# Differential-attention heads: rotary straight from PSUM, mask and row extreme in one VectorE operation, one sub-norm per head

## The chip, the cores and the metric

The program runs on one core of a Trainium2 chip. The metric is device microseconds of one execution. Five instruction queues run side by side and wait for one another through semaphores: TensorE (PE; its weight loads are listed apart as PEld), VectorE (DVE), ScalarE (ACT), GpSimd (POOL) and SyncE (SP, which here only issues DMAs). Every queue works strictly in its own order: an instruction that waits holds up all that stands behind it.

## The reference, cut to what matters

One decoder layer over 1024 tokens and a model width of 2048, all in float32. After an RMSNorm one input projection gives q, k, v and gate columns of two groups of eight heads: stick-breaking heads (not changed here) and differential heads. For a differential head:

```python
dq = partial_rope(df_q.reshape(qk_shape), pos)   # (B, S, 8 heads, 2, 64): two q/k pairs per head
dk = partial_rope(df_k.reshape(qk_shape), pos)   # rotates the first 16 of 64 dims: 8 with 8
s = einsum('bqhcd,bkhcd->bhcqk', qi, k) * 64 ** -0.5
pr = softmax(where(kpos <= qpos, s, -inf), axis=-1)
a = pr[:, :, 0] - lam * pr[:, :, 1]
df_out = rmsnorm(a @ v, subln_g, 1e-5) * (1 - lambda_init)
mixed = concat([sb_out * silu(sb_g), df_out * silu(df_g)])
```

An output projection, a gated per-layer embedding and a final RMSNorm follow.

## The kernel before, in words

The input comes in transposed, features on partitions, with the order of tokens turned round, so that the keys that a block of 128 queries may see lie at the end of a row. The tokens are worked in two halves of 512. A float32 product is made of three matmuls on a high and a low part of each operand (high·high, high·low, low·high), in the type fp32r. Before the heads, one stage computes the v and gate columns and puts them into DRAM (`vg_d`); behind the heads follow the output projection and the gate stage. Neither is touched.

The heads run in a fixed order: for half 1 the eight differential heads (8 to 15) and then the eight stick-breaking heads, then the same for half 0. Half 1 sees its own 512 keys alone; half 0 sees 1024. For each head `unit` makes the q and k columns: four weight pieces, each of eight groups of three matmuls of 512 columns, into two PSUM accumulators `acc0` (q) and `acc1` (k). A *tick* passes behind every group, 32 of them a head. All other work of a head hangs on ticks: `side.add([(t, fn)])` puts a step t ticks ahead, and steps that have come due are written into the program there. So the attention of one head is interleaved with the projection matmuls of the next, and **the order of the matmuls on PE is fixed in writing by tables of ticks** (`SC` for scores, `TT` for the transposes and the mixing, `ROPE`, `VGD`, `DF0`, `DF1`, `LM`, `LN`, `LAST`); on the other engines a scheduler orders the steps. PE never overtakes a matmul whose operand is late.

The way of a differential head, with the lines of the profile:

- **Rotation.** `taken` scales each accumulator by the row norm (and q by 64^-0.5) on DVE into SBUF (L1605 for q, L1609 for k). Only 16 of every 64 rows rotate, so SP DMAs gather the first 32 rows of both pairs of q and of k into one tile `rot` (L1612). DVE exchanges rows 0-7 with 8-15 (`stream_shuffle`, L1617), multiplies by sine and cosine (L1622, L1623) and adds (L1625). SP DMAs carry the rotated rows back (L1629).
- **Split and placing.** ACT casts to the high part (L1633); SP DMAs put the halves of it where the score matmuls want them: `q`, `qz` (the other 64 rows zero) and `k` (both copies) (L1636). DVE subtracts for the low part (L1642, L1646); two DMAs place q's low half (L1644). These are 18 DMA issues on SP per head, in the queue that also carries the weight pieces (L183, L184) and v and gate (L1513).
- **Scores.** Two matmuls give q·k (L338, L341; half 1: L427, L430) into a PSUM tile `z`; between them PE adds the causal mask as a bf16 matmul of an identity with a mask block (L340, L429). DVE reduces each row to minus its maximum (L388, L440), ACT takes exp with the row sum (L397, L444), DVE and ACT form the difference of the two softmaxes (L402 to L410, L447 to L452).
- **Mixing.** `turn` transposes the weights on PE into PSUM `tp` (L487), ACT and DVE split them (`awh` L505, `awl` L510, `lead` L504/L509), `mix` multiplies by v (L530 to L535) into PSUM `av`. `tp`, `av`, v's transpose and the sum of squares `msq` share one PSUM ring of two buffers.
- **Sub-norm.** For each half of a head's 512 queries PE sums squares into `msq` (L576, L577), ACT takes ln and exp of it (L604, L605), DVE makes one Newton step (L608 to L610, the first of them still reading `msq`) and scales (L611).
- **v and gate.** `load_vg` (L1513) reads them from DRAM; DVE multiplies both by the row norm (L1650), ACT makes the sigmoid of the gate.

In the order of the program of half 0, SP's queue stands so before the change, behind one weight piece (`whi`, `wlo`):

```order
L1612 DMA rot<-qk 32x512 x2
L304 DMA comb_d<-sg 128x512
L1629 DMA qk<-rot 32x512 x4
L183 DMA whi<-whi_d 128x1024
L184 DMA wlo<-wlo_d 128x1024
L1513 DMA vf<-vg_d 128x512
L1513 DMA gf<-vg_d 128x512
L1636 DMA q<-sw 64x512
L1636 DMA qz<-sw 64x512
```

The write-back of the rotated rows stands ahead of a weight piece and of v and gate.

Of the kernel before, what the change touches and what calls it, by code (L numbers as in the profile page):

```python
# [34 lines left out]
SC = ((20.5, 21, 23.5, 25.5, 29.5, 31.5, 34.0, 37.0), (24.5, 27, 34, 41))  # L35
TT = ((32, 44, 30.0), (35.5, 52, 33))
DGAP = (3, 6.5)
DF0 = (1, 1, 1.5, 3.5, 5.5)
DF1 = (1, 1.0, 3, 5, 6.5)
LV = ((2.0, 2.5), (1, 2))  # L40
LT = ((1, 1), (1, 2.0))
LM = ((0.5, 2.0, 3, 5), (1, 2, 4, 6))
LN = ((1, 4.0), (1, 4.5))
PRIO = 300
NORM_LAT = ((8, 7.0), (13, 11))
XLAT = 5
SBB = ((20, 20, 15, 16.0, 15, 16.5, 16.5, 16.0), (20, 9, 5.5, 4, 5.0, 6.0, 5.5, 4.0))
SBS = ((-1, 3.5, 15.5, 23.5), (0.5, 2, 7.5, 11.5))
SBT = ((15, 31, 11), (14.0, 27.5, 10.5))
SGAP = (3.5, 6.5)  # L50
SBL = ((1.5, 3, 6.0), (1, 3, 5.0))
SVG = ((18, 40.5, 42, 43, 49), (33.5, 34.5, 39.0, 40.0, 48.0))
ROPE = ((3.5, 4.0, 6.0, 10.0, 11.6, 12.5, 15.0), (6.5, 7, 9.5, 12.5, 12.6, 13.5, 14))
VGD = ((40, 47, 48, 49.0, 51.0), (37.5, 47.5, 47.5, 47.5, 55.5))
# [4 lines left out]
LAST = 2, 4.5  # L59
MASKPE = True  # L60
# [9 lines left out]
def _body(ctx, nc, tc, ap):  # L70
# [13 lines left out]
    masks = const.tile([P, 2, P], BF16, name="masks", tag="masks")  # L84
    identb = const.tile([P, P], BF16, name="identb", tag="identb")
# [14 lines left out]
    def consts_late():  # L100
        V.tensor_scalar(subg, subg, 1.0 - LAM0, None, op0=ALU.mult)
        V.tensor_copy(identb, ident)
# [207 lines left out]
    def attention(at, pz, half, hd, q, qz, K, KL, VV, sg, vg, state):  # L310
# [9 lines left out]

        def scores(c, rb):
# [5 lines left out]
            for ki, k in enumerate(K):  # L327
# [9 lines left out]
                else:  # L337
                    T.matmul(o, q[:, c, rs], k[:, c, c0:HALF], start=True, stop=False)  # L338
                    if ki == 0:
                        T.matmul(z[:, rs], identb, masks[:, 1, :], start=False, stop=False, skip_group_check=True)  # L340
                    T.matmul(o, qz[:, c, rs], KL[:, ki, c0:], start=False, stop=True)  # L341

            def masked():
                mask = masks[:, 0, :]
# [10 lines left out]
        def weights(rb, c):  # L355
# [30 lines left out]
            def top():  # L386
                mx = at.tile([P, 1], F32, name="mx", tag="mx", bufs=8)
                V.reduce_max(mx, z[:, vw], axis=AX.X, negate=True)  # L388
                side.later(DF0[2], partial(one, mx))

            def one(mx):
# [5 lines left out]
                A.activation(et[:, vw], z[:, vw], AF.Exp, bias=mx[:, 0:1], accum_out=l)  # L397
# [20 lines left out]
        def pairs(rb):  # L418
# [6 lines left out]
            for c in range(2):  # L425
                o = z[:, c, c0:]
                T.matmul(o, q[:, c, rs], k[:, c, c0:HALF], start=True, stop=False)  # L427
                if MASKPE:
                    T.matmul(z[:, c, rs], identb, masks[:, 1, :], start=False, stop=False, skip_group_check=True)  # L429
# [5 lines left out]
            def masked():  # L435
                mask = masks[:, 1:2, :].broadcast_to([P, 2, P])
                V.tensor_tensor(z[:, :, rs], z[:, :, rs], mask, op=ALU.add)

# [133 lines left out]
        def norm(pr):  # L572
# [5 lines left out]
            if hd == ORDER1[H - 1]:  # L578
# [4 lines left out]
                if pr == 0:  # L583
                    return
# [1843 lines left out]
```

## Time and profile before

| what | value |
|---|---|
| median of 3 runs | 2469.01 us (2468.71 to 2471.68) |
| the profiled execution | 2460.97 us, span 2459.2 us |
| granted clock over the span | 0.99 |
| busy share of the span | PE 96%, PEld 79%, DVE 71%, ACT 45%, POOL 14% |
| differential heads of half 1 (first to last q evacuated) | 644.1 to 869.1 us |
| stick-breaking heads of half 1 and the seam to half 0 | 869.1 to 1139.0 us |
| differential heads of half 0 | 1139.0 to 1431.1 us |
| stick-breaking heads of half 0 | 1431.1 to about 1800 us |

A row of the timeline has the start, the duration, the engine and line, the operation with its operands, and in brackets how long the engine had sat idle before it and what released it. A matmul's end is modelled, so that back-to-back matmuls overlap in the rows; what one costs is read from the distance of the starts.

### The profile page before, as it was taken

The page shows a single profiled execution, that of the slowest core. Times are in us where ns is not written, and L with a number is a line of the kernel's source. Part 1 is how long each engine was busy: PE and PEld are TensorE (multiplying, and loading weights), DVE is VectorE, ACT ScalarE, POOL GpSimd, SP SyncE. Part 2 cuts the span into 40 slices and gives each one's busy share as a digit, 9 for nine tenths or more (in the row PEclk, how much of TensorE's full clock was granted, in tenths as well). Part 3 has the DMA queues.
Part 4 walks back from the last instruction along what each step waited for, and adds up shares of the span by engine and source line. Part 5 has one row for each costly group of instructions (what it writes and reads, how often), then busy time and mean ns, then how long its engine had stood idle before and what let it go on. Part 6 is the DMA issues. An engine that isn't in the chain of part 4 may idle for free.

```text
span 2459.2 us, 33022 instructions
## 1 busy us (share of the span) xinstructions
PE 2358.3 (96%) x11230; PEld 1936.3 (79%) x11230; DVE 1754.9 (71%) x2954; ACT 1109.5 (45%) x2086; POOL 333.5 (14%) x496
## 2 busy tenths in 40 slices
PE   9999999999999989998999999999999999999997
PEld 7888878888777768886777778888878787778876
DVE  7589776666366767765677777767877886677688
ACT  6343243333244555443555555545632434532453
POOL 1211122223000000000010101110111222011000
PEclk9999999999999999999999999999999999999998
DMA  7797589999889888778687877667888899898965
GB/s 261 243 368 251 185 239 295 290 276 281 280 263 292 274 283 292 269 246 257 192 220 209 223 208 212 190 203 234 211 219 199 262 273 279 292 326 284 317 210 176
DMA packets 276457, 619.88 MB, mean 252 GB/s; under 512 B 33664, under 2 KB 45952, under 8 KB 276288
## 3 DMA queue, kind: packets, MB, share of 16 engines
q1 hardware_dynamic: 197328, 424.53, 53.2%
q0 software_dynamic: 59664, 158.10, 25.3%
q10 hardware_dynamic: 19296, 35.14, 4.1%
q8 instruction: 88, 1.44, 0.2%
q14 instruction: 81, 0.66, 0.1%
HBM read 374.37 MB, written 222.30 MB: 243 GB/s over the span
## 4 chain that ended last, share of the span: by engine, by line
PE 63%; DMA 16%; DVE 13%; ACT 4%; issue 3%; SPq 2%; DVEq 0%; ACTq 0%
PE pbc L726 6%; PE pbc L727 6%; PE pbc L728 6%; PE acc L262 5%; PE acc L264 5%; PE acc L263 5%; DMA rot<-qk 3%; PE pa L726 2%; PE pa L727 2%; PE pa L728 2%; PE tp L487 2%; DMA gf<-vg_d 2%; DMA q<-qk 1%; DMA wraw<-w_gate 1%; DMA wraw<-w_out 1%
## 5 line engine op out<-in xcount | busy, mean ns | idle before, releaser
L817 ACT CAST wpr<-T 128x512 fp32r<-128x512 f32 x208 | 125.4, 620 | 437.8 <-DVE T L782 358.3
L262 PE MATMUL acc<-xh,whi 128*128 128x512 f32 x768 | 314.2, 409 | 0.1
L264 PE MATMUL acc<-xh,wlo 128*128 128x512 f32 x768 | 303.0, 395 | 2.8 <-DVE wlo L195 2.5
L263 PE MATMUL acc<-xl,whi 128*128 128x512 f32 x768 | 301.5, 393 | 0.0
L264 PEld LDWEIGHTS acc<-xh,wlo 128*128 128x128 f32 x768 | 144.8, 189 | 37.1 <-DVE wlo L195 3.8
L263 PEld LDWEIGHTS acc<-xl,whi 128*128 128x128 f32 x768 | 145.7, 190 | 24.2
L262 PEld LDWEIGHTS acc<-xh,whi 128*128 128x128 f32 x768 | 145.7, 190 | 24.0 <-ACT whi L190 0.5
L817 ACT CAST wpr<-wraw 128x512 fp32r<-128x512 f32 x144 | 88.3, 616 | 153.5 <-DMA wraw<-w_vg 45.8
L831 DVE TENSOR_TENSOR wpr<-T,wpr 128x512 fp32r<-128x512 f32 x208 | 142.7, 686 | 11.3 <-ACT wpr L817 7.4
L950 POOL DMA_DIRECT2D vg_d<-hc x120 | 86.8, 724 | 331.1 <-DVE hc L1191 203.9
L510 DVE TENSOR_TENSOR awl<-tp,awh 128x256 fp32r<-128x256 f32 (+1 forms) x160 | 92.3, 577 | 46.0 <-ACT awh L505 45.8
L831 DVE TENSOR_TENSOR wpr<-wraw,wpr 128x512 fp32r<-128x512 f32 x144 | 97.8, 685 | 38.1 <-ACT wpr L817 38.0
L726 PE MATMUL pbc<-cS,wpr 128*128 128x512 f32 x288 | 112.2, 389 | 0.8 <-DVE u L1247 0.8
L728 PE MATMUL pbc<-cS,wpr 128*128 128x512 f32 x288 | 112.0, 389 | 0.0
L727 PE MATMUL pbc<-cS,wpr 128*128 128x512 f32 x288 | 112.0, 389 | 0.0
L505 ACT CAST awh<-tp 128x256 fp32r<-128x256 f32 (+1 forms) x160 | 80.4, 502 | 52.7 <-PE tp L487 44.9
L373 DVE TENSOR_TENSOR_SCAN st<-pt 128x511 f32<-128x511 f32 (+3 forms) x64 | 86.7, 1354 | 17.9 <-ACT pt L366 17.6
L388 DVE TENSOR_REDUCE mx<-z 128x1 f32<-128x1024 f32 (+3 forms) x64 | 65.2, 1018 | 32.7 <-PE z L341 32.6
L535 PE MATMUL av<-awl,v 128*128 128x256 f32 x256 | 74.9, 293 | 11.1 <-DVE awl L510 10.9
L366 ACT ACTIVATE pt<-z 128x512 f32<-128x512 f32 (+3 forms) x64 | 41.8, 653 | 88.8 <-DVE z L349 85.0
L397 ACT ACTIVATE et<-z,mx 128x1024 f32<-128x1024 f32 (+3 forms) x64 | 60.8, 952 | 31.9 <-DVE mx L388 31.9
L533 PE MATMUL av<-awh,v 128*128 128x256 f32 x256 | 72.6, 284 | 1.3 <-ACT awh L505 1.2
(579 smaller groups left out, 6798.7 us busy)
## 6 DMA issues: line engine op xcount, KB each, us to landing
wlo<-wlo_d SPq DMA_DIRECT2D x94, 512.0 KB, 5.2
whi<-whi_d SPq DMA_DIRECT2D x74, 512.0 KB, 4.1
wraw<-w_vg SPq DMA_DIRECT2D x130, 256.0 KB, 4.9
vg_d<-hc POOLq DMA_DIRECT2D x120, 256.0 KB, 5.8
wraw<-w_in SPq DMA_DIRECT2D x54, 512.0 KB, 5.4
wraw<-w_gate SPq DMA_DIRECT2D x92, 256.0 KB, 5.8
wraw<-w_out SPq DMA_DIRECT2D x72, 256.0 KB, 5.0
wlo_d<-wlo SPq DMA_DIRECT2D x34, 512.0 KB, 3.6
```

Of the source, the lines that this page charges most:

```text
L262: T.matmul(acc[c], hi[:, k2, kh, c, :], xh, start=first, stop=False)
L263: T.matmul(acc[c], hi[:, k2, kh, c, :], xl, start=False, stop=False)
L264: T.matmul(acc[c], lo[:, k2, kh, c, :], xh, start=False, stop=last)
L373: V.tensor_tensor_scan(st[:, off + 1:nkey], pt[:, off:nkey - 1], pt[:, off:nkey - 1], initial=1.0, op0=ALU.mult, op1=ALU.bypass)
L505: A.copy(wh[:, o, :], tp[:, o, :])
L510: V.tensor_tensor(wl[:, o, :], tp[:, o, :], wh[:, o, :].bitcast(F32), op=ALU.subtract)
L726: T.matmul(o, wh[:, w], xh, start=start and k == 0, stop=False, skip_group_check=True)
L727: T.matmul(o, wh[:, w], xl, start=False, stop=False, skip_group_check=True)
L728: T.matmul(o, wl[:, w], xh, start=False, stop=k == 3, skip_group_check=True)
L817: A.copy(t[:, 0], src)
L831: V.tensor_tensor(t[:, 1], src, t[:, 0].bitcast(F32), op=ALU.subtract)
L950: G.dma_start(vg_d[hf, blk, u], o, **(dict(accum_op=ALU.add) if ph else {}))
```

## The change

The table that `rope` loads (`cs`) is multiplied once per half by the row norm (two operations on 128x1024), so the rotation needs no norm of its own. For each head and each of q and k, DVE multiplies the accumulator by the cosine table straight from PSUM, shuffles the accumulator straight from PSUM, multiplies the shuffled copy by the sine table (zero where nothing rotates) and adds. All 128 rows go through, no row is moved. ACT writes q's and k's high parts in their places itself, 64 rows at a time (`high`, `spread`), and DVE writes q's low halves in their places (`low`). The 18 SP DMAs of a head are gone.

The mask matmul is gone too, and the scale 64^-0.5 with it out of q: one VectorE operation with an accumulator output (`tensor_tensor_reduce`) adds a mask row to the scores, multiplies by -64^-0.5, writes back to PSUM and gives the row's minimum; exp then runs with scale -1. In the order of the program it is two rows, the operation and the reading of its accumulator. In half 1 there is one for each of the two pairs, where one reduction took both.

The sub-norm takes both halves of a head together: ACT copies each `msq` out, then ln, exp and a square on 512 columns, and three DVE operations on 512 columns replace eight on 256.

The tick tables are other ones throughout; the table `VGD` asks for v and gate (first entry) and uses them (second and third) at other ticks than before.

```diff
-SC = ((20.5, 21, 23.5, 25.5, 29.5, 31.5, 34.0, 37.0), (24.5, 27, 34, 41))
-TT = ((32, 44, 30.0), (35.5, 52, 33))
+SC = ((6.5, 7, 9.0, 11.5, 15.5, 17.5, 20.0, 21.5), (10.5, 10.5, 15.5, 22.5))
+TT = ((19, 31, 17.5), (20.5, 36.5, 18))
...
-ROPE = ((3.5, 4.0, 6.0, 10.0, 11.6, 12.5, 15.0), (6.5, 7, 9.5, 12.5, 12.6, 13.5, 14))
-VGD = ((40, 47, 48, 49.0, 51.0), (37.5, 47.5, 47.5, 47.5, 55.5))
+CST = (19.5, 20)
+ROPE = ((-1.4, 1.5, 3.0, 3.5, 2.7, 4.5, 6.0, 7.0), (-1.9, -1, 0, 1, 0.20000000000000018, 2, 3, 4))
+VGD = ((31, 37, 37.0, 39.0, 41.0), (22.5, 32.5, 35.5, 37.0, 45.0))
...
+        def masked_top(z, n, mx):
+            V.tensor_tensor_reduce(z, z, mwide[:, 0:n], -DF_SCALE, 3.0e38, ALU.add, ALU.min, mx)
...
-                    if ki == 0:
-                        T.matmul(z[:, rs], identb, masks[:, 1, :], start=False, stop=False, skip_group_check=True)
...
-                V.reduce_max(mx, z[:, vw], axis=AX.X, negate=True)
+                masked_top(z[:, vw], nkey - off, mx)
...
-                A.activation(et[:, vw], z[:, vw], AF.Exp, bias=mx[:, 0:1], accum_out=l)
+                A.activation(et[:, vw], z[:, vw], AF.Exp, bias=mx[:, 0:1], scale=-1.0, accum_out=l)
...
-                V.reduce_max(mx, z[:, :, vw], axis=AX.X, negate=True)
+                for c in range(2):
+                    masked_top(z[:, c, vw], HALF - off, mx[:, c:c + 1])
...
+            if pr == 0:
+                sqs["both"] = [ev.tile([P, HALF], F32, name=nm, tag="sq", bufs=2) for nm in ("msqs", "rsub")]
+            m, r = sqs["both"]
+            side.later(LN[half][0], lambda: A.copy(m[:, ms_], msq))
+            if pr == 0:
+                return
...
             def step():
-                V.scalar_tensor_tensor(sq, msq, SUB_EPS, rs_, op0=ALU.add, op1=ALU.mult)
-                V.scalar_tensor_tensor(sq, sq, -0.5, rs_, op0=ALU.mult, op1=ALU.mult)
-                V.scalar_tensor_tensor(rs_, sq, 1.5, rs_, op0=ALU.add, op1=ALU.mult)
-                V.tensor_tensor(sg[:, ms_], sg[:, ms_], rs_, op=ALU.mult)
+                V.scalar_tensor_tensor(sg, sg, -0.5, r, op0=ALU.mult, op1=ALU.mult)
+                A.activation(r, r, AF.Square)
+                V.scalar_tensor_tensor(m, m, SUB_EPS, r, op0=ALU.add, op1=ALU.mult)
+                V.scalar_tensor_tensor(sg, m, -3.0, sg, op0=ALU.add, op1=ALU.mult)
...
+                if hd == (ORDER0, ORDER1)[half][0]:
+                    side.add([(CST[half], lambda cs=cs, rstd=rstd: V.tensor_tensor(cs, cs, rstd.rearrange("p (a n) -> p a n", a=1).broadcast_to([P, 2, HALF]), op=ALU.mult))])
...
-                            V.scalar_tensor_tensor(f, acc[c], DF_SCALE, rstd, op0=ALU.mult, op1=ALU.mult)
-                            V.tensor_tensor(f, acc[c], rstd, op=ALU.mult)
-                        for b in range(2):
-                            m = 64 * c + 32 * b
-                            nc.sync.dma_start(fs["r"].bitcast(F32)[m:m + 32, :], f[64 * b:64 * b + 32, :])
+                        f, sw = [t.bitcast(F32) for t in fs[c]]
+                        V.tensor_tensor(f, acc[c], cs[:, 0, :], op=ALU.mult)
+                        V.stream_shuffle(sw, acc[c], SWAP)
...
+                    def turned(c, fs=fs):
+                        f, sw = [t.bitcast(F32) for t in fs[c]]
+                        V.tensor_tensor(sw, sw, cs[:, 1, :], op=ALU.mult)
+                        V.tensor_tensor(f, f, sw, op=ALU.add)
+                    def high(c, fs=fs, qk=qk):
+                        f = fs[c][0].bitcast(F32)
+                        if c:
+                            A.copy(fs[1][1], f)
+                        for b, r in enumerate(rows):
+                            A.copy(qk[c][r, b, :], f[r])
+                    def low(c, fs=fs, qk=qk):
+                        f = fs[c][0].bitcast(F32)
+                        if c:
+                            V.tensor_tensor(qk["kl"][:, 0, :], f, fs[1][1].bitcast(F32), op=ALU.subtract)
                             return
                         for b, r in enumerate(rows):
+                            V.tensor_tensor(qk[0][rows[1 - b], b, :], f[r], qk[0][r, b, :].bitcast(F32), op=ALU.subtract)
+                    def spread(c, fs=fs, qk=qk, store_k=store_k, state=state):
+                        f = fs[c][0].bitcast(F32)
                         state.add("qk"[c])
+                        for b, r in enumerate(rows):
+                            if c:
+                                A.copy(qk[1][rows[1 - b], b, :], f[r])
+                            else:
+                                A.copy(qk["qz"][r, b, :], f[r])
+                        if c:
+                            store_k()
```

Three places of the new order, with the line numbers of the changed file. SP's queue in half 0 at the place that was shown before (`comb_d` is a store of an earlier head's result; L1491 loads v and gate):

```order
L184 DMA wlo<-wlo_d 128x1024
L304 DMA comb_d<-sg 128x512
L183 DMA whi<-whi_d 128x1024
L184 DMA wlo<-wlo_d 128x1024
L1491 DMA vf<-vg_d 128x512
L1491 DMA gf<-vg_d 128x512
```

No DMA of the rotation stands ahead of v and gate now, but the weight piece still does.

DVE's queue in half 1 from the k accumulator on (`acc_6302`) to the last thing that k's scores need (`kl`):

```order
L1587 TENSOR_TENSOR qk<-acc_6302,cs 128x512
L1588 STREAM_SHUFFLE sw<-acc_6302 128x512
L1608 TENSOR_TENSOR q<-qk,q 64x512 x2
L1592 TENSOR_TENSOR sw<-sw,cs 128x512
L1593 TENSOR_TENSOR qk<-qk,sw 128x512
L1622 TENSOR_TENSOR vf<-vf,ssa 128x512
L1605 TENSOR_TENSOR kl<-qk,sw 128x512
L1622 TENSOR_TENSOR gf<-gf,ssa 128x512
```

and ACT's queue at the same place:

```order
L499 CAST awh<-tp 128x512
L1600 CAST q<-qk 64x512 x2
L1617 CAST qz<-qk 64x512 x2
L1598 CAST sw<-qk 128x512
L1600 CAST k<-qk 64x512 x2
L1615 CAST k<-qk 64x512 x2
```

The work that SP's DMAs did now stands in these two queues, and `kl` stands behind the use of v (`vf`). On PE the first score matmul of this head now follows the last matmul of its k accumulator after 33 matmuls of 512 columns, six of 256 and three transposes; before, after 75 of 512, 21 of 256, 14 transposes and four mask matmuls. In half 0 it is 21 of 512, 17 of 256 and 11 transposes, from 69 of 512, 42 of 256, 26 transposes and three mask matmuls.

PE's queue at the scores of half 0, before the change:

```order
L338 MATMUL z<-k,q 128x384
L340 LDWEIGHTS identb
L340 MATMUL z<-masks,identb 128x128
L341 MATMUL z<-kl,qz 128x384
L338 MATMUL z<-k_10263,q 128x512
L341 MATMUL z<-kl,qz 128x512
```

and after it:

```order
L341 MATMUL z<-k,q 128x384
L342 MATMUL z<-kl,qz 128x384
L341 MATMUL z<-k_10146,q 128x512
L342 MATMUL z<-kl,qz 128x512
L524 MATMUL av<-lead,v 128x256 x2
```

Two instructions of PE's queue are gone at each of 128 places.

121 lines of the change are left out of this document (32 added, 89 removed).

## The prediction

> **What bounds the kernel now.** I read the page first: PE is busy nearly all the time, and the chain of waits that ended last lies on PE for the most part, then on DMA.
>
> ```profile
> PE 2358.3 (96%) x11230; PEld 1936.3 (79%) x11230; DVE 1754.9 (71%) x2954; ACT 1109.5 (45%) x2086; POOL 333.5 (14%) x496
> PE 63%; DMA 16%; DVE 13%; ACT 4%; issue 3%; SPq 2%; DVEq 0%; ACTq 0%
> ```
>
> So only what takes matmul time off PE, or idle time ahead of a matmul, can move the end. The windows by stage (length; busy of PE, PEld, DVE, ACT, POOL; granted clock; DMA) show where PE is not full: the stages with differential heads.
>
> ```profile
> core 0: us, PE busy (x) PEld busy (x) DVE busy (x) ACT busy (x) POOL busy (x), PEclk, DMA share, GB/s
> 200.00:250.00 50.00, 50.00 (x222) 41.39 (x222) 45.05 (x73) 19.75 (x34) 7.36 (x14) 1.00 0.71 229
> 644.10:869.10 225.00, 210.19 (x1042) 167.77 (x1040) 137.67 (x293) 97.31 (x256) 11.62 (x21) 0.98 0.89 276
> 1180.20:1431.10 250.90, 237.55 (x1265) 191.02 (x1263) 181.41 (x358) 134.75 (x267) 23.24 (x33) 1.00 0.77 213
> ```
>
> In half 1 seven head intervals fill 225.0 us (32.1 a head, DVE 19.7 of it); in half 0 six steady heads fill 250.9 (41.2 a head by the spacing of their q evacuations, DVE 29.8 of it). PE lacks 14.8 and 13.4 us there; the early stage shows PE full with DVE at 45.05 of 50.
>
> Third, PE's waits between 644 and 1500 us (who waited for whom: us in total, times, longest):
>
> ```profile
> PE tp L487 <- DVE sqv L608: 13.2, 13, 4.0
> PE z L427 <- DMA q<-qk: 10.8, 6, 5.1
> PE av L535 <- DVE awl L510: 10.2, 16, 2.1
> PE z L338 <- DMA q<-qk: 8.6, 6, 6.7
> PE av L530 <- DVE lead L509: 5.3, 3, 2.6
> ```
>
> Three kinds: scores waiting for the DMAs that place q and k (19.4), transposes waiting for a PSUM buffer that `msq` holds until the Newton step L608 (13.2), the mixing waiting for DVE (15.5). The timeline tells what lies behind them:
>
> ```profile
> 1157.56 0.62 ACT L1633 CAST sw<-qk 128x512 fp32r<-128x512 f32 x1 [11.28 <-DMA qk<-rot]
> 1167.86 0.80 PE L338 MATMUL z<-k,q 128*128 128x512 f32 x1 [6.73 <-DMA q<-qk]
> 915.35 0.90 PE L487 MATMUL tp<-ident,et 128*128 128x128 f32 x3 [3.99 <-DVE sqv L608]
> 1236.96 2.42 SPq L1629 DMA_DIRECT2D qk<-rot  x4
> 1241.02 0.43 SPq L1513 DMA_DIRECT2D gf<-vg_d  x1
> 1248.54 0.69 DVE L1650 TENSOR_TENSOR gf<-gf,ssa 128x512 f32<-128x512 f32 x1 [1.24 <-DMA gf<-vg_d]
> 1248.01 0.28 PE L533 MATMUL av<-awh,v 128*128 128x256 f32 x1
> 1248.12 0.28 PE L534 MATMUL av<-awh,v 128*128 128x256 f32 x1
> 1249.89 0.39 PE L535 MATMUL av<-awl,v 128*128 128x256 f32 x1 [1.49 <-DVE awl L510]
> ```
>
> The rotation's round trips stop ACT for 11.28 us and then PE for 6.73. In half 0 the mixing waits for a DVE that waits for the gate `gf`, landing 7.5 us after its issue (1241.02 to 1248.54). After the longest waits PE also runs slow for a while:
>
> ```profile
> 1167.00:1174.00 7.00, 6.14 (x17) 4.41 (x18) 1.95 (x2) 1.21 (x2) 0.00 (x0) 0.58 0.31 114
> 911.00:920.00 9.00, 4.75 (x14) 3.28 (x13) 7.67 (x17) 5.00 (x13) 1.07 (x2) 0.64 0.60 218
> ```
>
> A clock of 0.58 over 7.0 us loses 2.9 us, 0.64 over 9.0 us 3.2.
>
> **The change part by part. The mask matmul.** 128 of them go.
>
> ```profile
> 1299.94 0.33 PE L338 MATMUL z<-k,q 128*128 128x384 f32 x1
> 1300.11 0.23 PE L340 MATMUL z<-masks,identb 128*128 128x128 bf16 x1
> 1300.15 0.42 PE L341 MATMUL z<-kl,qz 128*128 128x384 f32 x1
> 1300.41 0.39 PE L338 MATMUL z<-k,q 128*128 128x512 f32 x1
> 1300.63 0.39 PE L341 MATMUL z<-kl,qz 128*128 128x512 f32 x1
> L340 PE MATMUL z<-masks,identb 128*128 128x128 bf16 x64 | 15.0, 234 | 0.0
> L429 PE MATMUL z<-masks,identb 128*128 128x128 bf16 x64 | 14.9, 233 | 0.0
> ```
>
> By starts, L338 on 384 columns takes 0.17 us, the mask 0.04, and the L341 behind it, on as many columns, 0.26 instead of 0.17: the mask costs 0.04 + 0.09 = 0.13. At 0.12 to 0.13 each, 128 make 15.4 to 16.6; I take **-15.4**.
>
> The busy sums of the two rows would give 29.9. [...]
>
> ```profile
> L340 PEld LDWEIGHTS <-identb 128*128 128x128 bf16 x64 | 6.3, 98 | 10.7 <-issue 10.0
> ```
>
> [...]
>
> **The DMA waits.** With the 18 DMAs per head the wait of 19.4 goes. Each of its 12 waits hides a further 0.16, because a matmul of 0.39 in the rows starts its successor after 0.23: 1.9. Clock after the two longest (5.1, 6.7): two times 2.9, near 6. Together **-27**.
>
> **The PSUM wait.** `msq` is freed by a copy one tick behind its matmul, no longer by L608 on a busy DVE: 13.2, hidden 13 x 0.16 = 2.1, clock near 5 (3.2 at 915, less at the shorter ones): **-20**.
>
> **The wait for v and gate** stays, I think. SP no longer holds them behind the write-back, but they follow a weight piece still, and half 0's table asks 6 ticks ahead (31 to 37) where it asked 7 (40 to 47). Six ticks of a 37 us head are 6.9 us, against the 7.5 seen. The row L1650 still stands before DVE's next split in half 0, and PE's mixing behind that. I take 0; the bounds are -18.5 (15.5 and 19 x 0.16: all goes) and +6 (8 steady heads by 0.7, the difference).
>
> **DVE and ACT per head.** The rows that price it (mean ns behind the comma):
>
> ```profile
> L1609 DVE TENSOR_TENSOR qk<-acc,ssa 128x512 f32<-128x512 f32 x15 | 10.3, 687 | 1.7 <-PE acc L264 1.4
> L1617 DVE STREAM_SHUFFLE sw<-rot 128x512 f32<-128x512 f32 x16 | 11.8, 735 | 0.1
> L1623 DVE TENSOR_TENSOR rot<-rot,cs 128x512 f32<-128x512 f32 x16 | 11.0, 685 | 0.0
> L388 DVE TENSOR_REDUCE mx<-z 128x1 f32<-128x1024 f32 x16 | 19.6, 1225 | 30.3 <-PE z L341 30.3
> L378 DVE TENSOR_TENSOR bt<-st,bt 128x1023 f32<-128x1023 f32 x8 | 9.7, 1216 | 0.0
> L402 DVE RECIPROCAL l<-l 128x1 f32<-128x1 f32 x64 | 9.9, 155 | 2.5 <-ACT et L397 2.5
> L608 DVE SCALAR_TENSOR_TENSOR sqv<-msq,rsub 128x256 f32<-128x256 f32 x28 | 11.6, 414 | 0.0
> L1633 ACT CAST sw<-qk 128x512 fp32r<-128x512 f32 x16 | 9.9, 619 | 41.1 <-DMA qk<-rot 41.0
> ```
>
> Rotation: 8 operations become 11, +2.1 us. Sub-norm: 8 x 0.414 become 3 x 0.69, -1.2. The new masked minimum is not in the trace. It streams two operands like L378 and reduces like L388; both run 1024 columns in 1.22, so at one pass it costs what L388 did, plus an accumulator read (near 0.16, the shortest DVE row): 8 x 0.16 = +1.3 a head. At two passes it costs their sum, 2.44. One pass is my value, since a single operand stream sets both rows. DVE then needs 29.8 + 2.2 = 32.0 of a half 0 head of about 37 (86%), and some 22.5 of 28 in half 1: under the 90% at which PE was full in the early stage. ACT gains 7 casts (+4.3) and 1 us of norm per head, on 45% busy; its cover is PE's stream. The two multiplications of the table (1.2 us each) hide under a head's matmuls, at tick 19.5 with the use at 28. POOL's stores of k wait for ACT's casts instead of the DMAs; no PE wait above has POOL behind it. Nothing here is on PE's path by itself: 0.
>
> [...]
>
> **The new, shorter way to the scores.** Between the end of k's accumulator and the head's first score PE now has 33 x 0.23 + 6 x 0.12 + 3 transposes = 8.6 us of other work in half 1, and 21 x 0.23 + 17 x 0.12 + 11 x 0.1 = 8.0 in half 0 (0.12: 1248.01 to 1248.12 lies between two of 256 columns); before it was over 21. In that time DVE must run 0.687 + 0.735 + 2 x 0.687 (q's low) + 2 x 0.685 = 4.2 us, then ACT five casts, 3.1: 7.3 without any delay, and in half 0 three shorter operations of the value path stand between. Every lag of DVE beyond about 1 us is a PE wait. Bounds: 0, and 3 us a head (48). I take 0.7 a head, 16 heads, **+11**, nearer to 0 because the sum fits.
>
> Sum: -15.4 - 27 - 20 + 0 + 11 = -51. The profiled execution took 2460.97, so 2410; the median of the runs lies 8.0 above it (2469.01), so **2418**.
>
> **The rivals.**
> - *More goes.* No new wait, and the wait for v and gate goes too: -15.4 - 27 - 20 - 18.5 = -81, 2388. For it: SP's queue is empty of the rotation. Against: the weight piece in front.
> - *DVE becomes the bound.* At two passes a half 0 head (6656 columns of minima) needs 32.0 + 7.9 = 39.9 us of DVE, at the 90% of the early row 44.3: +3.1 for 8 heads, 25. Half 1 stays PE-bound: -7.7 - 27 - 20 + 6 = -49. Net -24, 2445.
> - *Waits only move.* The stalls come back in full at other matmuls, since PE's order is written out; only the mask stays: 2454.
> - *Slower: the shortened way to the scores decides.* From 4 us of wait a head on (62 / 16) it eats all that was gained. Its place is the first score matmul: `kl` stands behind the use of v in half 1, so a late v (7.5 us seen) delays it, and ACT's five casts stand behind the splits of the last head. At 6 us: 2461 - 62 + 96 = 2495, 2503 in the median. Against: the 7.3 us fit into 8.6.
> - *It does nothing*: PE's 96% is an artefact and something else ends last; the chain with 63% on PE speaks against it.
>
> **How the numbers follow.** Forecast 0.58 (own range 2400 to 2435), more goes 0.15, DVE bound 0.10, waits move 0.08, nothing 0.02, slower 0.07. Faster by over 0.2% (about what a measurement of this kernel can tell from no change) are the first four, 0.91, less 0.02 for waits that come back longer than they were: 0.89; same 0.02 and these 0.02: 0.04; slower 0.07. The range from 2385 to 2447 takes in the first three and leaves out the last three, some 0.17.
>
> **What would show it.** Right: no PE row of the scores waits for a DMA; `tp` no longer waits for the norm; the score matmuls lie 0.17 and 0.17 apart; half 1 heads near 28.5 us, half 0 heads near 38.5. Wrong: the masked minimum at over 2 us on 1024 columns; a wait of several us ahead of each head's first score; DVE idle ahead of v longer than before; a clock under 0.9 in these stages.

## The result and the profile after

The changed kernel takes 2391.74 us (median of 4 runs, 2383.89 to 2396.24) beside 2468.86 for the kernel before (4 runs): a ratio of 0.9687, 95% interval 0.9655 to 0.9720. The forecast was 2418. In a later comparison on one chip it took 2387.18 (5 runs, 2385.73 to 2388.53), ratio 0.9677 (0.9656 to 0.9699). The profiled execution shown here took 2393.9 us, its span is 2392.1; before they were 2460.97 and 2459.2, so 67 us less.

The page of the changed kernel, engines and then the chain of waits that ended last:

```profile
PE 2332.3 (97%) x11102; PEld 1936.5 (81%) x11102; DVE 1781.2 (74%) x3107; ACT 1189.3 (50%) x2213; POOL 334.3 (14%) x497
PE 72%; DVE 11%; DMA 8%; ACT 7%; issue 2%; SPq 0%; ACTq 0%; DVEq 0%
```

DMA halves its share of the chain (16% before), PE goes from 63% to 72%. The windows by stage (length; busy of PE, PEld, DVE, ACT, POOL; clock; DMA share; GB/s), half 1 and half 0, each from the first q evacuation to the last:

```profile
648.70:853.10 204.40, 202.01 (x1014) 168.82 (x1013) 159.52 (x403) 140.18 (x337) 12.51 (x23) 1.00 0.73 246
1112.40:1375.20 262.80, 260.23 (x1385) 219.06 (x1385) 219.37 (x463) 189.06 (x361) 28.36 (x39) 1.00 0.62 191
```

Seven head intervals of half 1 now take 204.4 us (225.0 before), seven of half 0 take 262.8 (292.1 before, from 1139.0 to 1431.1), with DVE at 78% and 83% and PE at 99%. That is 50 of the 67 us. The stretch between the two (it begins with the last differential head of half 1) went from 269.9 to 259.3 us, that behind them from 1028.1 to 1017.0, and the part ahead of the heads took 4.6 more. Of PE's waits from 640 to 1500 us, five of the twelve rows (us in total, times, longest):

```profile
PE z L428 <- ACT et L440: 3.3, 4, 1.7
PE z L337 <- ACT k L1557: 1.7, 1, 1.7
PE av L529 <- DVE awl L504: 1.3, 5, 0.3
PE z L341 <- ACT k L1615: 0.9, 1, 0.9
PE av L524 <- DVE lead L503: 0.3, 1, 0.3
```

All three kinds of waits of the kernel before are gone: for q's DMAs (19.4), for the norm (13.2) and, which I had not forecast, for the splits of the mixing (15.5, now 1.6). All rows of this view come to 55.4 us before and 14.1 now. What stood in the gate's way before shows in the timeline of half 0:

```profile
1220.60 0.99 SPq L1491 DMA_DIRECT2D gf<-vg_d  x1
1232.67 0.68 DVE L504 TENSOR_TENSOR awl<-tp,awh 128x512 fp32r<-128x512 f32 x1
1234.20 0.69 DVE L1622 TENSOR_TENSOR vf<-vf,ssa 128x512 f32<-128x512 f32 x1
1234.80 0.69 DVE L1622 TENSOR_TENSOR gf<-gf,ssa 128x512 f32<-128x512 f32 x1
```

The gate is asked for 14 us ahead of its use; before it was 7.5 with DVE waiting. The new operations cost what the rows of before had said (groups of DVE by shape, mean ns behind the comma):

```profile
L1588 DVE STREAM_SHUFFLE sw<-acc 128x512 f32<-128x512 f32 x32 | 23.6, 738 | 0.0
L1587 DVE TENSOR_TENSOR qk<-acc,cs 128x512 f32<-128x512 f32 x32 | 21.9, 685 | 10.8 <-PE acc L264 10.7
L322 DVE CUSTOM_DVE_ANT_0 z<-z,masks 128x1024 f32<-128x1024 f32 x16 | 19.7, 1229 | 1.5 <-PE z L342 0.8
L322 DVE DVE_READ_ACCUMULATOR2_ANT mx<- 128x1 f32 x128 | 18.2, 142 | 0.0
```

Adding the mask, scaling and taking the row minimum of 1024 columns is one pass: 1229 ns, beside 1225 for the plain reduction before.

### The profile page after: what moved, and what is told of

The parts are those of the page before. It is cut to its first block, busy times and chain, and to the rows that moved or that the text cites. A ratio compares the mean times of both kernels' runs of the same rounds, so it can differ in the third digit from the quotient of the medians.

```text
span 2392.1 us, 32521 instructions
## 1 busy us (share of the span) xinstructions
PE 2332.3 (97%) x11102; PEld 1936.5 (81%) x11102; DVE 1781.2 (74%) x3107; ACT 1189.3 (50%) x2213; POOL 334.3 (14%) x497
## 4 chain that ended last, share of the span: by engine, by line
PE 72%; DVE 11%; DMA 8%; ACT 7%; issue 2%; SPq 0%; ACTq 0%; DVEq 0%
PE acc L262 7%; PE acc L264 7%; PE acc L263 7%; PE pbc L703 6%; PE pbc L705 6%; PE pbc L704 6%; PE pa L705 2%; PE pa L704 2%; PE pa L703 2%; PE tp L481 2%; DMA wraw<-w_gate 1%; DMA wraw<-w_out 1%; PE pb L1918 1%; PE pb L704 1%; PE pb L705 1%
## 5 line engine op out<-in xcount | busy, mean ns | idle before, releaser
L264 PE MATMUL acc<-xh,wlo 128*128 128x512 f32 x768 | 302.3, 394 | 1.1 <-DMA wlo<-wlo_d 1.1
L264 PEld LDWEIGHTS acc<-xh,wlo 128*128 128x128 f32 x768 | 144.4, 188 | 35.0 <-DMA wlo<-wlo_d 2.3
L808 DVE TENSOR_TENSOR wpr<-wraw,wpr 128x512 fp32r<-128x512 f32 x144 | 97.9, 686 | 38.6 <-ACT wpr L794 38.5
L504 DVE TENSOR_TENSOR awl<-tp,awh 128x256 fp32r<-128x256 f32 (+1 forms) x160 | 92.5, 578 | 43.0 <-ACT awh L499 42.2
L322 DVE CUSTOM_DVE_ANT_0 z<-z,masks 128x512 f32<-128x512 f32 (+7 forms) x128 | 97.1, 769 | 22.9 <-PE z L342 13.8
L367 ACT ACTIVATE pt<-z 128x512 f32<-128x512 f32 (+3 forms) x64 | 41.8, 653 | 76.9 <-DVE z L350 74.9
L527 PE MATMUL av<-awh,v 128*128 128x256 f32 x256 | 72.0, 281 | 0.7 <-ACT awh L499 0.7
L528 PE MATMUL av<-awh,v 128*128 128x256 f32 x256 | 72.2, 282 | 0.0
```

Source lines behind the costliest of these rows:

```text
L264: T.matmul(acc[c], lo[:, k2, kh, c, :], xh, start=False, stop=last)
L322: V.tensor_tensor_reduce(z, z, mwide[:, 0:n], -DF_SCALE, 3.0e38, ALU.add, ALU.min, mx)
L504: V.tensor_tensor(wl[:, o, :], tp[:, o, :], wh[:, o, :].bitcast(F32), op=ALU.subtract)
L808: V.tensor_tensor(t[:, 1], src, t[:, 0].bitcast(F32), op=ALU.subtract)
```

## The experiments

Two directions: one part of the change alone on the kernel before, and the changed kernel with one thing taken back. The last column but one is the mean distance between the q evacuations of neighbouring heads in the steady part, four intervals of half 1 and six of half 0; the last is the sum of PE's visible waits from 640 to 1500 us.

| kernel | median us | ratio to before (95%) | profiled span | head, half 1 / half 0 | waits |
|---|---|---|---|---|---|
| before | 2468.86 | 1 | 2459.2 | 31.8 / 41.8 | 55.4 |
| e2 mask alone | 2467.85 | 1.0016 (1.0005 to 1.0028) | 2465.4 | 33.2 / 41.5 | 64.0 |
| e3 norm alone | 2479.24 | 1.0060 (1.0045 to 1.0075) | 2476.9 | 34.9 / 41.2 | 61.8 |
| e4 rotation alone | 2484.39 | 1.0081 (1.0062 to 1.0101) | 2482.9 | 35.9 / 45.5 | 69.1 |
| e5 early gate alone | 2471.91 | 1.0024 (1.0008 to 1.0039) | 2473.9 | 31.7 / 42.6 | 61.6 |
| e6 all parts, old tables | 2474.94 | 1.0032 (1.0017 to 1.0047) | 2474.0 | 34.6 / 43.9 | 73.4 |
| e9 e6, 14 ticks earlier | 2477.06 | 1.0046 (1.0029 to 1.0064) | 2475.3 | 34.2 / 43.5 | 75.9 |
| e10 e6, 7 ticks earlier | 2465.22 | 0.9998 (0.9988 to 1.0009) | 2463.3 | 37.6 / 40.5 | 62.0 |
| e11 e6, rotation spread | 2475.15 | 1.0032 (1.0010 to 1.0055) | 2473.4 | 35.6 / 43.6 | 69.2 |
| after | 2387.18 | 0.9677 (0.9656 to 0.9699) | 2386.0 | 29.1 / 37.9 | 13.8 |
| e1 mask on PE again | 2396.95 | 0.9720 (0.9697 to 0.9742) | 2393.2 | 29.5 / 38.9 | 12.9 |
| e8 two ticks moved | 2397.06 | 0.9717 (0.9696 to 0.9739) | 2395.5 | 30.2 / 38.1 | 19.6 |
| e12 norm put back | 2399.90 | 0.9736 (0.9719 to 0.9752) | 2399.1 | 29.4 / 39.0 | 26.7 |

The kernel before was measured anew beside each group of runs; its medians were 2464.20 (e2 to e5), 2467.50 (after, e1, e6, e8) and 2464.32 (e9 to e12).

### One part alone, on the kernel before

**e2, the mask.**

```diff
-                    if ki == 0:
-                        T.matmul(z[:, rs], identb, masks[:, 1, :], start=False, stop=False, skip_group_check=True)
...
-                V.reduce_max(mx, z[:, vw], axis=AX.X, negate=True)
+                V.tensor_tensor_reduce(z[:, vw], z[:, vw], mwide[:, 0:n], -1.0, 3.0e38, ALU.add, ALU.min, mx)
```

> The kernel before with one part of the change alone: the 128 mask matmuls go, and one VectorE operation adds the mask, changes the sign and takes the row minimum. Rotation, norm and the order of the heads stay. By the starts (0.12 to 0.13 us a mask matmul) it takes about 15 us off, 2453 to 2456 in the median and near 2445 profiled. Rival by the busy sums of the two mask rows: 30 us, near 2439. Rival 'the DVE operation pays it back' (142 ns of accumulator read behind each minimum, ahead of waits that PE already has): 0 to -5 us, 2464 and more.

Measured: no gain, 1.0016. The 128 matmuls are gone, and PE waits as much longer (waits of this kernel from 640 to 1500 us):

```profile
PE tp L480 <- DVE sqv L601: 19.7, 18, 4.5
PE z L427 <- DMA q<-qk: 12.5, 8, 5.1
```

13 waits of the transposes for the norm have become 18, 13.2 us have become 19.7. Heads of half 0 got 0.3 us shorter, those of half 1 1.4 longer. So in the old order the exchange is worth nothing, which is the number of the rival *the DVE operation pays it back*. Two causes fit: PE's own work did not set the length of a head there, or DVE's 128 new accumulator reads (142 ns each in the rows above) ate the gain. This run does not separate them.

**e3, the norm.**

```diff
+            side.later(LN[half][0], lambda: A.copy(m[:, ms_], msq))
+            if pr == 0:
+                return
...
-                V.scalar_tensor_tensor(sq, msq, SUB_EPS, rs_, op0=ALU.add, op1=ALU.mult)
...
+                V.scalar_tensor_tensor(sg, sg, -0.5, r, op0=ALU.mult, op1=ALU.mult)
```

> The kernel before with one norm a head alone: msq is copied out of PSUM one tick behind its matmul, and the Newton step runs once on 512 columns. If the wait of tp for sqv was a cost of its own, it takes 13 us (the visible wait) to 20 us (with what hides behind pipelining and the clock after the longest waits) off: 2449 to 2456, and no row tp <- DVE sqv is left. Rival 'the stall moves on', since PE's order is written out and the next matmul waits for the same DVE: 0 to -5 us, with longer waits at av <- awl or at z <- q in the same heads.

Measured: slower, 1.0060. The wait that it was to remove is gone, and others have grown by more (waits of PE from 640 to 1500 us):

```profile
PE z L427 <- DMA q<-qk: 24.3, 7, 4.9
PE av L530 <- DVE lead L509: 12.0, 10, 2.6
```

No row `tp <- sqv` is left, as expected; the scores of half 1 wait 24.3 us for their DMAs instead of 10.8. Heads of half 1 got 3.1 us longer, those of half 0 0.6 shorter. Neither expectation had a loss of 15 us.

**e4, the rotation**, with all ticks of the kernel before except those of the rotation itself. Because the scale leaves q and the mask stays on PE, this run has something that neither kernel has: behind each reduction one more small DVE operation scales the row extreme.

```diff
-                            V.scalar_tensor_tensor(f, acc[c], DF_SCALE, rstd, op0=ALU.mult, op1=ALU.mult)
...
-                            nc.sync.dma_start(fs["r"].bitcast(F32)[m:m + 32, :], f[64 * b:64 * b + 32, :])
...
+                        V.tensor_tensor(f, acc[c], cs[:, 0, :], op=ALU.mult)
+                        V.stream_shuffle(sw, acc[c], SWAP)
```

> The kernel before with the rotation alone: read from PSUM, norm in the table, no transfer of rows; the scale goes into the exponential. All ticks of the scores, the mixing and the loads are those of before. Theory 'the queue held v and the gate': the waits of z for the DMAs go (19.4 visible, 27 with clock) and also the waits of the mixing (15.5), because nothing in SP's queue stands ahead of v and gate any more: -40 to -48 us, 2421 to 2429, and gate issued 10 us or more ahead of its use. Rival 'ticks': the loads still come seven ticks ahead of their use, the mixing waits stay, -25 to -30 us, 2439 to 2444. Rival 'waits only move': under -15 us.

Measured: slower, 1.0081. The waits of PE from 640 to 1500 us:

```profile
PE tp L490 <- DVE sqv L611: 41.9, 13, 4.1
PE av L536 <- ACT awh L508: 14.1, 7, 2.5
PE av L538 <- DVE awl L513: 1.3, 6, 0.2
```

No score waits for a DMA any more (19.4 before) and the splits wait 1.3 us for DVE instead of 10.2: both causes are removed. But 13 transposes, as many as before, now wait 41.9 us for the norm instead of 13.2, 3.2 us each. The time went to the next place at which PE's written order meets DVE. Part of the loss may be the run's own: the 96 added operations, at the 0.15 us of each row in half 0 (L390, 1216 to 1269 us), come to an estimated 14 us of DVE. None of the three forecasts had a loss.

The run also tells what made the load of v and gate early or late. Nothing of the rotation stands in SP's queue any more, and the entries of `VGD` are the old ones:

```profile
1245.38 0.32 SPq L184 DMA_DIRECT2D whi<-whi_d  x1
1246.70 0.42 SPq L1516 DMA_DIRECT2D gf<-vg_d  x1
1253.85 0.68 DVE L1647 TENSOR_TENSOR gf<-gf,ssa 128x512 f32<-128x512 f32 x1
```

I had expected 10 us or more between the gate's issue and its use; it is 7.2, no more than before (7.5). The gate goes right behind a weight piece, and such a piece waits for PE (in the changed kernel L183 for `acc` L264: 59 waits of 315.2 us from 640 to 1500 us). It is in time all the same: the row of its use, 7.2 us behind the issue, shows no wait.

**e5, v and gate** asked for seven ticks earlier in half 0, ahead of the rotation's write-back in SP's queue.

```diff
-VGD = ((40, 47, 48, 49.0, 51.0), (37.5, 47.5, 47.5, 47.5, 55.5))
+VGD = ((33, 47, 48, 49.0, 51.0), (37.5, 47.5, 47.5, 47.5, 55.5))
```

> The kernel before with one number changed: in half 0 v and gate are asked for at tick 33 instead of 40, ahead of the rotation's write-back in SP's queue. If the place behind that write-back is what made them late, the waits of the mixing for DVE in half 0 go: -10 to -15 us, 2454 to 2459. If the landing itself (5 to 6 us) or DVE's load made them late, no change within 4 us. If the loads now stand ahead of the write-back and hold it up, z waits longer for q: slower by up to 5 us.

The timeline at one gate of half 0, and the waits of PE from 640 to 1500 us:

```profile
1230.74 0.42 SPq L1513 DMA_DIRECT2D gf<-vg_d  x1
1252.05 0.68 DVE L1650 TENSOR_TENSOR gf<-gf,ssa 128x512 f32<-128x512 f32 x1
```

```profile
PE av L533 <- ACT awh L505: 12.0, 7, 2.2
PE av L535 <- DVE awl L510: 3.7, 7, 0.5
```

The gate is now issued 21 us ahead of its use, and DVE does not wait for it. The seven ticks put it ahead of both the write-back and one weight piece; which of the two held it up, this run alone does not tell. The wait of the splits for DVE falls from 10.2 to 3.7 us, and a wait of the same products for ACT's cast `awh` rises from 0.5 to 12.0. Measured 1.0024: nothing gained.

### All parts, on the tables of before

**e6** has every operation of the changed kernel, and of the new tables only those without which they cannot stand: ROPE, CST (the multiplication of the cosine table) and LAST.

```diff
-SC = ((6.5, 7, 9.0, 11.5, 15.5, 17.5, 20.0, 21.5), (10.5, 10.5, 15.5, 22.5))
-TT = ((19, 31, 17.5), (20.5, 36.5, 18))
+SC = ((20.5, 21, 23.5, 25.5, 29.5, 31.5, 34.0, 37.0), (24.5, 27, 34, 41))
+TT = ((32, 44, 30.0), (35.5, 52, 33))
...
-VGD = ((31, 37, 37.0, 39.0, 41.0), (22.5, 32.5, 35.5, 37.0, 45.0))
+VGD = ((40, 47, 48, 49.0, 51.0), (37.5, 47.5, 47.5, 47.5, 55.5))
```

(DGAP, DF0, LV, LM, LN, NORM_LAT and the tables of the stick-breaking heads go back too.)

> The changed kernel's operations with all tables of ticks of the kernel before (scores at tick 20.5 and later, v and gate seven ticks ahead of use, over 21 us between k's accumulator and the first score). If the short way to the scores costs what I had forecast (0.7 us a head), this is as fast or up to 11 us faster than the changed kernel, less what the other ticks gave. If the short way costs nothing and the tables are only an adjustment, it is within 5 us of it. Rival 'the gain is in the ticks': slower than the changed kernel by 15 us or more, with waits of the mixing or of the scores back.

Measured 2474.94, 88 us slower than the changed kernel on the same chip and 1.0032 of the kernel before. The thought that the tables are only an adjustment falls: with the same operations, the whole gain hangs on the tables. Of the 88 us, 54 lie in the fourteen head intervals of the two differential stages, 15 between the stages and 19 behind them, where the tables of the stick-breaking heads went back as well. PE's waits from 640 to 1500 us:

```profile
PE tp L481 <- DVE et L448: 24.5, 8, 3.3
PE av L524 <- DVE lead L503: 22.8, 9, 2.6
PE av L527 <- ACT awh L499: 12.6, 7, 2.7
```

The timeline of half 1 shows one of the first kind. DVE works without a gap from 736.22 to 746.5, and the difference of two softmaxes, for which a transpose stands on PE, comes only behind the next head's rotation: its factor (L444) stands there on DVE, ACT's L445 needs that factor, and L448 needs L445:

```profile
745.26 0.69 DVE L1593 TENSOR_TENSOR qk<-qk,sw 128x512 f32<-128x512 f32 x1
746.39 0.16 DVE L444 TENSOR_TENSOR l<-l,lam 128x1 f32<-128x1 f32 x1
747.30 0.62 DVE L448 SCALAR_TENSOR_TENSOR et<-et,l 128x384 f32<-128x384 f32 x1 [0.74 <-ACT et L445]
747.97 0.33 PE L481 MATMUL tp<-ident,et 128*128 128x128 f32 x1 [3.17 <-DVE et L448]
```

From this I formed a theory: in the old tables a head's softmax falls into the same ticks as the next head's rotation, and the new ones pull them apart by 14 ticks (the score ticks of half 0 are the old ones less 14, but for two of eight, by 0.5 and 1.5). Three runs tested it.

**e9 and e10**: e6 with SC, TT and VGD less 14, and less 7.

```diff
-SC = ((20.5, 21, 23.5, 25.5, 29.5, 31.5, 34.0, 37.0), (24.5, 27, 34, 41))
-TT = ((32, 44, 30.0), (35.5, 52, 33))
+SC = ((6.5, 7, 9.5, 11.5, 15.5, 17.5, 20.0, 23.0), (10.5, 13, 20, 27))
+TT = ((18, 30, 16.0), (21.5, 38, 19))
```

> The changed kernel's operations with the tables of the kernel before (the run e6_old_ticks, 2475), except that scores, mixing and the loads of v and gate all stand exactly 14 ticks earlier (SC, TT, VGD minus 14, nothing tuned). Theory 'phase': in the old tables the softmax and the mixing of a head fall into the same ticks as the next head's rotation, which keeps DVE full for 12 us; shifted by 14 ticks they fall ahead of it. Then most of the 88 us between e6 and the changed kernel come back: 2390 to 2410. Theory 'fine tuning': the gain is in the single half ticks of the new tables, 2440 or more.

> As e9_shift14, with a shift of 7 ticks instead of 14. Theory 'phase': half of the way, part of the softmax still meets the rotation: 2415 to 2450. If any way shorter than 21 us would do (only the distance counts, not the meeting with the rotation), about as e9. Theory 'fine tuning': as e6, 2465 or more.

**e11**: e6 with the rotation's steps spread over 15 ticks.

```diff
-ROPE = ((-1.4, 1.5, 3.0, 3.5, 2.7, 4.5, 6.0, 7.0), (-1.9, -1, 0, 1, 0.20000000000000018, 2, 3, 4))
+ROPE = ((-1.4, 3.5, 6.5, 8.5, 5.0, 10.5, 12.5, 14.0), (-1.9, 2, 5, 7, 4, 8, 10, 12))
```

> The changed kernel's operations with all tables of the kernel before (e6_old_ticks, 2475), but the rotation's steps spread over 15 ticks, as its round trips spread them in the kernel before, instead of 8; the scores come late enough for that. If the full 12 us of DVE behind q's evacuation are what delays the last head's mixing in e6 (tp for et 24.5, av for lead 22.8), these waits shrink by half or more: 2440 to 2460. Rival 'DVE's burst is not the cause': within 6 us of 2475.

The theory that a shift of 14 ticks brings the gain fell. So shifted the kernel takes 2477.06, no better than e6; by 7 it takes 2465.22, with heads of half 0 3.4 us shorter than in e6 and heads of half 1 3.0 us longer. The waits of e9, then of e10, then of e11:

```profile
PE tp L481 <- DVE et L448: 22.6, 14, 2.3
PE av L529 <- DVE awl L504: 13.1, 7, 1.9
```

```profile
PE av L527 <- ACT awh L499: 31.5, 13, 5.8
```

```profile
PE av L524 <- DVE lead L503: 22.8, 9, 2.6
PE av L527 <- ACT awh L499: 19.7, 13, 2.8
PE tp L481 <- DVE et L448: 9.4, 8, 1.4
```

Spreading the rotation did to the wait that I had named what I expected (24.5 to 9.4 us) and to the time nothing: `awh` took over 7.1 of it, and the sum of all waits fell only from 73.4 to 69.2. The heads keep the same distance for most of a stage (44.1, 44.1, 44.1, 44.0 in half 0 of e9; 37.7, 37.6, 37.6, 37.6 in half 1 of e10), so the waits come back alike in every head. I read them as a round that PE, ACT and DVE turn once per head: who removes one wait finds the next link of the same round. The runs agree with this reading; they do not prove it.

E9 is not the new order but for half ticks. In the changed kernel three of the four score entries of half 1 stand 16.5 to 18.5 ticks ahead of the old ones instead of 14, and in half 0 the entries of `VGD` stand 3 to 5 ticks behind those of e9.

What a few ticks do can be seen at one place in half 0 of e9, where v and gate are used at ticks 33 and 34 instead of 37. DVE's queue there, and the product that waits for L504:

```profile
1282.94 0.68 DVE L1622 TENSOR_TENSOR vf<-vf,ssa 128x512 f32<-128x512 f32 x1
1283.54 0.48 DVE L552 SCALAR_TENSOR_TENSOR sg<-sm,subg,sg 128x256 f32<-128x256 f32 x1
...
1286.81 0.69 DVE L1622 TENSOR_TENSOR gf<-gf,ssa 128x512 f32<-128x512 f32 x1
1287.42 0.68 DVE L504 TENSOR_TENSOR awl<-tp,awh 128x512 fp32r<-128x512 f32 x1
1288.16 0.39 PE L529 MATMUL av<-awl,v 128*128 128x256 f32 x1 [1.87 <-DVE awl L504]
```

The products of v and gate with the row norm stand ahead of the split that PE waits for; in the changed kernel (its rows above, 1232.67 to 1234.80) both stand behind it. Each holds DVE for 0.6 us (1282.94 to 1283.54, 1286.81 to 1287.42), so by these rows they make an estimated 1.2 of the 1.87 us of this wait. DVE is as full there in the changed kernel as on the old tables: of the first quarter of a steady head of half 0, counted from q's evacuation, it works 93% of the time in the changed kernel and in e6 alike. What differs is which of its work comes first.

### The changed kernel with one thing taken back

**after_again**, for comparison on the same chip.

> The changed kernel itself, beside the three that are derived from it, on the same chip: 2384 to 2396, ratio to the kernel before 0.966 to 0.972.

**e1, the mask back on PE** (it is then added twice, by PE and by DVE).

```diff
+                    if ki == 0:
+                        T.matmul(z[:, rs], identb, masks[:, P:2 * P], start=False, stop=False, skip_group_check=True)
                     T.matmul(o, qz[:, c, rs], KL[:, ki, c0:], start=False, stop=True)
```

> The changed kernel with the 128 mask matmuls put back on PE (the mask is then added twice, by PE and by DVE; the result is the same). By the starts in the trace it costs 0.12 to 0.13 us each, +15.4 to +16.6 us against the changed kernel of the same call. Rivals: by the busy sums +30; by the weight loads of the mask rows +12.5; hidden in PE's remaining waits, under +5.

Measured 2396.95 beside 2387.18: 9.8 us. The starts say the same price as before the change:

```profile
1198.66 0.40 PE L343 MATMUL z<-k,q 128*128 128x512 f32 x1
1198.89 0.23 PE L345 MATMUL z<-masks,identb 128*128 128x128 bf16 x1
1198.93 0.48 PE L346 MATMUL z<-kl,qz 128*128 128x512 f32 x1
1199.25 0.40 PE L343 MATMUL z<-k,q 128*128 128x512 f32 x1
```

0.04 to the next start and 0.32 instead of 0.23 behind it, 0.13 in all, 16.6 for 128. Heads of half 0 are 1.0 longer, which is what eight masks at 0.13 make; heads of half 1 only 0.4, and there the wait of z L428 for ACT falls (3.3 to 1.9 us). So in the new order a mask matmul is paid at its price where PE is full, and partly hidden where a wait is left; in the old order (e2) its exchange was worth nothing.

**e12, the norm of before put back** in the new order.

```diff
+            if hd != ORDER1[H - 1]:
+                rs_ = ev.tile([P, 2 * P], F32, name="rsub", tag="sm", bufs=5)
...
+                side.later(LN[half][0], roots)
+                side.later((4.0, 4.5)[half], step)
+                return
```

> The changed kernel with the norm of the kernel before put back for all heads but the last of half 1 (roots and Newton step on each 256 columns, msq held in PSUM until the step). If one norm a head is worth in the new order what its wait was in the old, +13 to +20 us, 2400 to 2410, with tp <- DVE sqv back. Rival 'the new order has room for it': within 4 us of the changed kernel (2387 to 2392).

Measured 2399.90, ratio 0.9736 beside 0.9677 of the changed kernel, which was measured on another chip: 0.6%, some 14 us (13 by the profiled spans); by the two intervals it may be 7 us more or less. In this order the norm is worth about the lower end of what I had expected, and the wait returns by name: `tp <- DVE sqv` 7.6 us in 9 times.

**e8, two entries of the score table**, to remove the longest kind of wait that is left.

```diff
-SC = ((6.5, 7, 9.0, 11.5, 15.5, 17.5, 20.0, 21.5), (10.5, 10.5, 15.5, 22.5))
+SC = ((6.5, 7, 9.0, 11.5, 15.5, 17.5, 20.0, 21.5), (10.5, 10.5, 17.5, 23.5))
```

> The changed kernel with the third and fourth score block of half 1 two ticks and one tick later (17.5 and 23.5 instead of 15.5 and 22.5). It is aimed at the longest wait that is left in half 1, z L428 for ACT's exponential (3.3 us in four waits). If that wait stands alone, -3 us (0.13%), which only the profiles can tell; if the scores come too late for the mixing behind them, +2 to +5 us.

The waits of PE from 640 to 1500 us:

```profile
PE av L524 <- DVE lead L503: 4.5, 7, 0.8
PE msq L570 <- DVE v L466: 3.5, 2, 1.7
PE z L428 <- ACT et L440: 0.3, 1, 0.3
```

The wait goes as meant (3.3 to 0.3), two others come (8.0 us against 0.3), and the kernel takes 9.9 us more (ratios 0.9717 and 0.9677). A tick or two at two places cost twice the most that I had expected. Nothing that I ran beats the changed kernel.

## Why the prediction was right or wrong

The direction and the outer range (2385 to 2447) held; the range named for the forecast itself (2400 to 2435) did not. The forecast gain of 51 us was short of the measured 77 in the medians and 67 in the profiles, and the reason behind it was right only for the operations together with their new tables.

- **What bounds the kernel.** Right that the loss lay in PE's waits in the differential stages: 50 of the 67 us came there. In the table of experiments time goes with the waits: among the kernels without mask matmuls the profiled span goes from 2386.0 at 13.8 us of visible waits to 2474.0 at 73.4, some 1.5 us of time for one of visible wait (1.4 to 1.6 for most of them, 1.0 for e12). That is the ratio of the prediction's terms too (13.2 visible to 20 with hidden part and clock).
- **The mask, -15.4.** Mis-sized. The price by starts came again (0.13 each); what it was worth was 10 us in the new order and nothing in the old one (there together with DVE's new reads). The estimate by weight loads (128 of 98 ns) gave 12.5. Both lie above the 9.8, and the remaining waits that took up part of it keep this run from telling them apart; the 30 of the busy sums is out.
- **The DMA waits, -27.** The waits went (no score waits for a DMA in the changed kernel). But that the waits go is not enough to win their time: in e4 the same DMAs are gone, the same 19.4 us of waits are gone, and the kernel is slower by 20 us, of which the operations that this run adds may be a part. What the rotation alone is worth in the new order stays open; no run takes it back there.
- **The PSUM wait, -20.** e12 gives some 14 in the new order (20 is not excluded by the two intervals), e3 a loss of 15 in the old one.
- **The wait for v and gate, 0.** Wrong: it went. I had counted the ticks between load and use in the table (six, 6.9 us) as the time between issue and use; it was 14. What counts is the place in SP's queue. That the rotation's DMAs are gone does not by itself bring the gate forward: e4 has none of them either, keeps the old entries, and issues the gate 7.2 us ahead of its use. In both kernels SP issues v and gate right behind a weight piece, and the new entry puts them behind an earlier one: in e4 they follow a piece that goes 19 us after q's evacuation (1226.34 to 1245.38), in the changed kernel one that goes 4.8 us ahead of it (1218.64 to 1223.43). The wait itself is gone in e4 and e5 too. What its end is worth in the new order no run shows; in the old order it was worth nothing (e5). The bound for this case, -18.5, was in the prediction.
- **DVE and ACT at 0 on the path.** The durations were right: one pass (1229 ns, 142 for the read), 685 and 738 from PSUM. On 128x512 the rows show no price of reading from PSUM: the shuffle takes 738 ns from PSUM (L1588) and took 735 from SBUF (L1617 before), the product takes 685 from PSUM (L1587) and 686 from SBUF (L1592). But "nothing here is on PE's path" holds only for the new order; in e6 the same operations stand in front of what PE waits for.
- **The shorter way, +11.** Mis-sized. In the changed kernel the scores of the differential heads wait for k once, 0.9 us at the first head of half 0 (L337 belongs to the stick-breaking heads); a steady head has no such wait. The forecast of 7.3 us held: in one head of half 1 the last cast of k ends 7.3 us after the accumulator's first reading starts (736.12 to 743.44), half a microsecond ahead of the first score (743.94).
- **The sum.** With the wait for v and gate at -18.5 and the short way at +0.9 the terms give -80; the mask at 10 instead of 15.4 makes that -75, and the new waits of z L428 and L337 (5.0 us, 7.5 by the factor of 1.5) -67. That this meets the 67 of the profiles is partly luck: the 27 and the 18.5 are measured by no run, and with the 14 of e12 in the place of the 20 the sum is -61. The terms are values in this order only and not additive in any other.
- **The rivals.** *More goes* (2388) is what came by its number, and the wait that it named did go. Its reason, an SP queue empty of the rotation, is not shown to have made the time: e4 has that queue too and is slower. *DVE becomes the bound* fell with one pass. *Waits only move*, to which I gave 0.08, is untrue of the change, and describes each part alone, all parts on the old tables, and the attempts to mend those tables by one rule (e10 alone gained there, some 8 us on e6 by the ratios). *Slower* did not come. Heads of 29.1 and 37.9 us stand beside the 28.5 and 38.5 forecast.

What I left out altogether is that the diff rewrites a dozen tables of ticks, and that these rows are a part of the change like its operations. I read them only for distances (6 ticks, 8.6 us of cover). What stays open: which of the other entries matter beside the one place shown, what of the gain the tables of the stick-breaking heads carry, and whether the operations of before could gain by tables of their own.

## What to carry to other kernels

Where an order written out by hand makes one engine wait for another several times a head, a visible wait is no price of its own: removing its cause can move it to the next place of the same round until the order is written anew for the new durations; here it did so in e3, e4 and e5. So judge a part of such a change in the order in which it will run, and take it back there (here 10 and 14 us), rather than add it alone to the old order (here 0 and a loss of 15). A load's lead over its use is read from the issuing queue, by what stands ahead of it and waits (here a weight piece), not from the distance in the program's table.

## What the runs showed of the hardware that I had not expected

- One microsecond of visible PE wait goes with some 1.5 us of time here, over the eight kernels without mask matmuls. One part of it can be seen: in e6 the matmuls of 512 columns behind the wait of 3.17 us start 0.41 to 0.43 us apart for 3.4 us (748.05 to 751.44), instead of 0.23. In the kernel before they start 0.42 to 0.43 us apart behind its wait of 6.73 us (1169.12 to 1171.26), and the granted clock is 0.58 from 1167 to 1174 us. That the clock and the pipelined part of a matmul make up all of the rest is not shown. The first starts in e6:

```profile
748.05 0.60 PE L262 MATMUL acc<-cA11h,whi 128*128 128x512 f32 x1
748.46 0.63 PE L263 MATMUL acc<-cA11l,whi 128*128 128x512 f32 x1
748.88 0.63 PE L264 MATMUL acc<-cA11h,wlo 128*128 128x512 f32 x1
```

- An early transfer was nothing won by itself: in e5 the uses of the gate at 1210.82 and 1252.05 us have no wait in their rows, and the time does not change for the better (1.0024).
- Half the rows cost the whole time: an operation on 64x512 took 686 ns on DVE (L1608) and 617 to 620 on ACT (L1600, L1615, L1617), one on 128x512 took 685 (L1587) and 622 (L1598). So placing q and k by halves, as the engines do now in place of the DMAs, costs twice what a whole tile would.
